# Rotary embedding on one core: the sine table is asked for ahead of the first two rows

## The chip, the core and the metric

The kernel runs on one core of a Trainium2 chip. Of the core's engines it uses VectorE (DVE in the profile) for the arithmetic, ScalarE (ACT) for a few conversions between float32 and float16, GpSimd (POOL) to issue most of the DMAs, and SyncE (SP) to issue the others. The core has 16 DMA engines, which all its DMAs share. TensorE (PE) has no work. The metric is the device time of one execution in microseconds (us); less is better.

## The reference

The input x has the shape (8, 2048, 16, 64) in float32: batch, position, head, and 64 numbers per head. The tables cos and sin have the shape (2048, 32). Each head's 64 numbers are two halves of 32, which are rotated against each other by the angle of the position:

```python
x1 = x[..., :head_dim // 2]
x2 = x[..., head_dim // 2:]
cos = cos[None, :, None, :]
sin = sin[None, :, None, :]
out1 = x1 * cos - x2 * sin
out2 = x1 * sin + x2 * cos
return np.concatenate([out1, out2], axis=-1)
```

x and the output have 67.1 MB each, a table 256 KB. Three operations per number of x stand against one read and one write of it.

## The kernel before, in words

**Tiles.** The 2048 positions of a batch are laid on 128 partitions, 16 consecutive positions ("rows", j) on each. A batch is one tile `xt` of 128 x 16 x 16 x 64 in float16 (4096 KB); five such buffers exist (`NBUF = 5`), so that batch b and batch b + 5 share one. The load (line 52) converts float32 to float16 on its way, and the stores (lines 60, 100, 130, 132) convert back.

**Arithmetic.** `rotate` makes three VectorE instructions per batch: line 73 multiplies the swapped halves with the sine table, whose first half has its sign turned (`v`), line 79 multiplies the tile in place with the cosine table, and line 81 adds `v`. The tables that VectorE reads, `sin_h` and `cos_h`, are float16. ScalarE makes them from the float32 tables: `sin_h` in two instructions (lines 88 and 89), `cos_h` in one (line 90).

**The head.** The first two rows of batch 0 (`JA = 2`, 1024 KB of float32) come by a way of their own. SyncE loads them in float32 into the tile `head` (line 36), and ScalarE converts them into the buffer of batch 0 (line 84). POOL's load of batch 0 brings only rows 2 to 15. `rotate` is called for rows 0 and 1 first, and then for rows 2 to 15. At the end of the kernel the tile `head` is used once more: ScalarE converts the last two rows of batch 7 into it (line 140), and SyncE stores them (line 141) behind the part of batch 7 that line 130 stores.

**Queues.** SyncE issues four DMAs, in the order head, sine table, cosine table, and the last rows at the end. The profile calls their queue q1 (hardware_dynamic). POOL issues everything else, and that queue is q0 (software_dynamic). POOL's order is: the loads of batches 0 to 3; the store of row 0 of batch 0 (line 100); the load of batch 4; the stores of batch 0 from row 1 on and of batch 1; the loads of batches 5 and 6; the stores of batches 2 and 3; the load of batch 7; the stores of batches 4 to 6; and batch 7 in two parts, rows 0 to 8 (line 130) and rows 9 to 13 (line 132). A load into a buffer that is used again waits until the store out of it has landed. A store waits for the last addition (line 81) of its rows.

Within q1 each DMA is cut into pieces of one row of memory per partition: 8192 bytes for the head, 2048 bytes for a table, eight pieces on each of the 16 DMA engines. In q0 a load's piece is counted at the float16 it writes (28672 bytes for batch 0, 32768 for the others).

Of the kernel before, what the change touches and what calls it, by code (L numbers as in the profile page):

```python
# [1 line left out]

# [4 lines left out]


@with_exitstack  # L10
def kernel(
    ctx: ExitStack,
    tc: tile.TileContext,
    x: bass.AP,
    cos: bass.AP,
    sin: bass.AP,
    out: bass.AP,
):
    nc = tc.nc
    f16 = mybir.dt.float16  # L20
    f32 = mybir.dt.float32

    B, S, H, D = x.shape
    Dh = D // 2
    P = nc.NUM_PARTITIONS
    J = S // P
    NBUF = 5

    const_pool = ctx.enter_context(tc.tile_pool(name="rope_const", bufs=1))
    io_pool = ctx.enter_context(tc.tile_pool(name="rope_io", bufs=NBUF))  # L30
    tmp_pool = ctx.enter_context(tc.tile_pool(name="rope_tmp", bufs=1))

    JA = 2
    head = const_pool.tile([P, JA, H, D], f32)
    x0 = x[0].rearrange("(p j) h d -> p j (h d)", j=J)
    nc.sync.dma_start(  # L36
        out=head.rearrange("p j h d -> p (j h d)"),
        in_=x0[:, 0:JA, :].rearrange("p j f -> p (j f)"),
    )
    sin_f = const_pool.tile([P, J, Dh], f32)  # L40
    cos_f = const_pool.tile([P, J, Dh], f32)
    cos_h = const_pool.tile([P, J, Dh], f16)
    sin_h = const_pool.tile([P, J, D], f16)
    nc.sync.dma_start(out=sin_f, in_=sin.rearrange("(p j) d -> p j d", j=J))  # L44
    nc.sync.dma_start(out=cos_f, in_=cos.rearrange("(p j) d -> p j d", j=J))

    loads = []

    def load(b):
        xt = io_pool.tile([P, J, H, D], f16)  # L50
        j0 = JA if b == 0 else 0
        dma = nc.gpsimd.dma_start(  # L52
            out=xt[:, j0:J, :, :].rearrange("p j h d -> p (j h d)"),
            in_=x[b].rearrange("(p j) h d -> p j (h d)", j=J)[:, j0:J, :].rearrange("p j f -> p (j f)"),
        )
        loads.append(dma)
        return xt

    def store(b, xt, j0=0):
        return nc.gpsimd.dma_start(  # L60
            out=out[b].rearrange("(p j) h d -> p j (h d)", j=J)[:, j0:J, :].rearrange("p j f -> p (j f)"),
            in_=xt[:, j0:J, :, :].rearrange("p j h d -> p (j h d)"),
        )

    def rotate(xt, j0, j1):
        v = tmp_pool.tile([P, J, H, D], f16)
        n = j1 - j0
        js = slice(j0, j1)
        shape = [P, n, H, 2, Dh]
        sin_b = sin_h[:, js, :].rearrange("p j (e d) -> p j e d", e=2).unsqueeze(2).to_broadcast(shape)  # L70
        cos_b = cos_h[:, js, :].unsqueeze(2).to_broadcast([P, n, 2 * H, Dh])
        xe = xt[:, js, :, :].rearrange("p j h (e d) -> p j h e d", e=2)
        nc.vector.tensor_mul(  # L73
            out=v[:, js, :, :].rearrange("p j h (e d) -> p j h e d", e=2),
            in0=xe[:, :, :, ::-1, :],
            in1=sin_b,
        )
        xw = xt[:, js, :, :].rearrange("p j h (e d) -> p j (h e) d", d=Dh)
        nc.vector.tensor_mul(out=xw, in0=xw, in1=cos_b)  # L79
        xa = xt[:, js, :, :].rearrange("p j h d -> p (j h d)")  # L80
        nc.vector.tensor_add(out=xa, in0=xa, in1=v[:, js, :, :].rearrange("p j h d -> p (j h d)"))  # L81

    tiles = [load(b) for b in range(NBUF - 1)]
    nc.scalar.copy(  # L84
        out=tiles[0][:, 0:JA, :, :].rearrange("p j h d -> p (j h d)"),
        in_=head.rearrange("p j h d -> p (j h d)"),
    )
    nc.scalar.copy(out=sin_h[:, :, Dh:D], in_=sin_f)  # L88
    nc.scalar.mul(out=sin_h[:, :, 0:Dh], in_=sin_f, mul=-1.0)  # L89
    nc.scalar.copy(out=cos_h, in_=cos_f)  # L90
    rotate(tiles[0], 0, JA)
    def part(b, j0, j1):
        return (
            out[b].rearrange("(p j) h d -> p j (h d)", j=J)[:, j0:j1, :].rearrange("p j f -> p (j f)"),
            tiles[b][:, j0:j1, :, :].rearrange("p j h d -> p (j h d)"),
        )

    def store_rows(b, j0, j1):
        dst, src = part(b, j0, j1)
        return nc.gpsimd.dma_start(out=dst, in_=src)  # L100

    first = store_rows(0, 0, 1)
    tc.add_manual_dep(
        first.ins,
        loads[NBUF - 2].ins.name,
        mybir.DependencyInfo(mybir.DependencyClass.NoSync, mybir.DependencyReason.DATA),
        reason="order of the ring",
    )
    tiles.append(load(NBUF - 1))
    tc.add_manual_dep(  # L110
        loads[NBUF - 1].ins,
        first.ins.name,
        mybir.DependencyInfo(mybir.DependencyClass.NoSync, mybir.DependencyReason.DATA),
        reason="order of the ring",
    )
    for b in range(B):
        rotate(tiles[b], JA if b == 0 else 0, J)
        if b < B - 1:
            st = store(b, tiles[b], 1 if b == 0 else 0)
            if b == 0:  # L120
                tc.add_manual_dep(
                    st.ins,
                    first.ins.name,
                    mybir.DependencyInfo(mybir.DependencyClass.NoSync, mybir.DependencyReason.DATA),
                    reason="order of the ring",
                )
        if b + NBUF < B:
            tiles.append(load(b + NBUF))
    dst, src = part(B - 1, 0, 9)
    gate = nc.gpsimd.dma_start(out=dst, in_=src)  # L130
    dst, src = part(B - 1, 9, J - JA)
    rest = nc.gpsimd.dma_start(out=dst, in_=src)  # L132
    tc.add_manual_dep(
        rest.ins,
        gate.ins.name,
        mybir.DependencyInfo(mybir.DependencyClass.NoSync, mybir.DependencyReason.DATA),
        reason="order of the ring",
    )
    dst, src = part(B - 1, J - JA, J)
    nc.scalar.copy(out=head.rearrange("p j h d -> p (j h d)"), in_=src)  # L140
    end = nc.sync.dma_start(out=dst, in_=head.rearrange("p j h d -> p (j h d)"))
    tc.add_manual_dep(
        end.ins,
        gate.ins.name,
        mybir.DependencyInfo(mybir.DependencyClass.Sync, mybir.DependencyReason.DATA),
        reason="the last rows go out behind this part",
    )


# [1 line left out]
_INS = ['x', 'cos', 'sin']  # L151
_OUTS = [((8, 2048, 16, 64), 'float32')]


# [23 lines left out]
```

## Time and profile before

| | |
|---|---|
| time, median of 3 runs | 317.52 us (316.82 to 317.85) |
| profiled execution, first to last instruction (span) | 315.70 us |
| outside the span, median less span | 1.82 us |
| VectorE busy | 209.1 us in 27 instructions |
| ScalarE busy | 6.8 us |
| POOL busy | 9.9 us |
| moved by q0 (counted at the destination) | 99.09 MB |
| moved by q1 (counted at the destination) | 2.62 MB |
| read from HBM, written to HBM | 67.63 MB, 67.11 MB |
| issue to landing: head, sine table, cosine table | 4.8, 13.5 and 32.0 us |

The profiled execution has no time of its own beside its span: what the device time has more, the start ahead of the first instruction and the end behind the last one, is taken as the difference to the median of the runs.

A page of the profile gives busy times, shares of the DMA engines in slices of the span, the chain of work that ended last, and groups of instructions with the idle time before them and what ended that. The DMA share of a stretch is the time of all DMA pieces that start in it, divided by 16 engines and by the length of the stretch. It can be a little over 1, because a piece is counted where it starts and neighbouring pieces of one engine overlap by some hundredths of a us. A share near 1 means that no DMA engine stood still. "Another core or an unknown queue" in the chain is time for which the profile found no releaser.

### The profile page before, as it was taken

To read this page: it belongs to the slowest core of one execution; us is meant where nothing else is said; L and a number is where in the kernel's file an instruction comes from. 1 tells how busy PE (TensorE), PEld (TensorE's weight loads), DVE (VectorE), ACT (ScalarE), POOL (GpSimd) and SP (SyncE) were. 2 spreads that over 40 slices of the span, in tenths; PEclk is the share of its full clock that TensorE was granted. 3 is DMA by queue.
4 is the path that set the end of the run, shared out by engine and by line. 5 is a ranking of instruction groups with operands and counts; after the bars stand their busy time and mean duration, and the time that the engine had idled before them with its cause. 6 is when DMAs were issued, how large, how long until landed. Compare 5 with 4: busy or idle time off the path is not lost.

```text
span 315.7 us, 122 instructions
## 1 busy us (share of the span) xinstructions
DVE 209.1 (66%) x27; ACT 6.8 (2%) x6; POOL 9.9 (3%) x22
## 2 busy tenths in 40 slices
DVE  0010699999999999999999999994009994000000
ACT  4100000000000000000000000000000002000000
POOL 3000100000000000001000000100000001000000
DMA  9899999999999989999999999999999999999998
GB/s 277 183 262 208 199 220 245 199 199 199 266 199 199 498 374 523 399 332 241 224 199 199 390 407 399 399 531 266 199 249 482 399 399 515 415 399 399 432 434 330
DMA packets 3168, 101.71 MB, mean 322 GB/s; under 512 B 352, under 2 KB 352, under 8 KB 736
## 3 DMA queue, kind: packets, MB, share of 16 engines
q0 software_dynamic: 2592, 99.09, 98.1%
q1 hardware_dynamic: 576, 2.62, 2.3%
HBM read 67.63 MB, written 67.11 MB: 427 GB/s over the span
## 4 chain that ended last, share of the span: by engine, by line
DVE 25%; DMA 22%; issue 18%; another core or an unknown queue 17%; POOL 1%; ACT 1%; SPq 0%; POOLq 0%; DVEq 0%; ACTq 0%
DMA xt<-in_x_dram 12%; DMA cos_f<-in_cos_dram 10%; DVE xt L79 8%; DVE xt L81 8%; DVE v L73 8%; ACT head L140 1%; POOL out_dram L60 1%; POOL xt L52 0%; ACT cos_h L90 0%; SPq L44 0%; SPq L36 0%; POOLq L52 0%; POOLq L60 0%; DVEq L73 0%
## 5 line engine op out<-in xcount | busy, mean ns | idle before, releaser
L73 DVE TENSOR_TENSOR v<-xt,sin_h 128x16384 f16<-128x16384 f16 (+2 forms) x9 | 69.7, 7744 | 36.8 <-DMA xt<-in_x_dram 20.7
L79 DVE TENSOR_TENSOR xt<-xt,cos_h 128x16384 f16<-128x16384 f16 (+2 forms) x9 | 69.7, 7744 | 17.5 <-ACT cos_h L90 17.2
L81 DVE TENSOR_TENSOR xt<-xt,v 128x16384 f16<-128x16384 f16 (+2 forms) x9 | 69.7, 7744 | 0.3
L52 POOL DMA_DIRECT2D xt<-in_x_dram x8 | 4.4, 557 | 111.1 <-DMA out_dram<-xt 110.3
L140 ACT CAST head<-xt 128x2048 f32<-128x2048 f16 x1 | 1.9, 1897 | 229.5 <-DVE xt L81 229.5
L60 POOL DMA_DIRECT2D out_dram<-xt x7 | 3.7, 535 | 63.9 <-DVE xt L81 63.9
L130 POOL DMA_DIRECT2D out_dram<-xt x1 | 0.5, 531 | 46.3 <-DVE xt L81 46.3
L84 ACT CAST xt<-head 128x2048 f16<-128x2048 f32 x1 | 1.9, 1897 | 3.6 <-DMA head<-in_x_dram 3.6
L100 POOL DMA_DIRECT2D out_dram<-xt x1 | 0.5, 541 | 33.5 <-DVE xt L81 33.5
L84 ACT ACT_TABLE_LOAD x1 | 1.3, 1283 | 0.7 <-PEq L162 0.7
L90 ACT CAST cos_h<-cos_f 128x512 f16<-128x512 f32 x1 | 0.6, 618 | 17.8 <-DMA cos_f<-in_cos_dram 17.8
L88 ACT CAST sin_h<-sin_f 128x512 f16<-128x512 f32 x1 | 0.6, 617 | 7.2 <-DMA sin_f<-in_sin_dram 7.2
L89 ACT ACTIVATE sin_h<-sin_f 128x512 f16<-128x512 f32 x1 | 0.6, 624 | 0.0
L132 POOL DMA_DIRECT2D out_dram<-xt x1 | 0.5, 531 | 0.0
L162 POOL MEMSET const-float32-0.0<- 128x1 f32 x1 | 0.1, 99 | 0.2 <-issue 0.2
L162 POOL MEMSET const-bfloat16-1.0<- 128x1 bf16 x1 | 0.1, 102 | 0.0
L162 POOL MEMSET const-float32-1.0<- 128x1 f32 x1 | 0.1, 99 | 0.0
L162 POOL MEMSET const-uint8-127<- 128x1 uint8 x1 | 0.1, 99 | 0.0
## 6 DMA issues: line engine op xcount, KB each, us to landing
xt<-in_x_dram POOLq DMA_DIRECT2D x7, 4096.0 KB, 41.3
out_dram<-xt POOLq DMA_DIRECT2D x1, 7680.0 KB, 61.6
out_dram<-xt POOLq DMA_DIRECT2D x1, 4608.0 KB, 42.4
xt<-in_x_dram POOLq DMA_DIRECT2D x1, 3584.0 KB, 22.3
out_dram<-xt POOLq DMA_DIRECT2D x1, 2560.0 KB, 47.9
head<-in_x_dram SPq DMA_DIRECT2D x1, 1024.0 KB, 4.8
out_dram<-head SPq DMA_DIRECT2D x1, 1024.0 KB, 8.4
out_dram<-xt POOLq DMA_DIRECT2D x1, 512.0 KB, 47.1
```

The source lines that it names most:

```text
L52: dma = nc.gpsimd.dma_start(out=xt[:, j0:J, :, :].rearrange("p j h d -> p (j h d)"), in_=x[b].rearrange("(p j) h d -> p j (h d)", j=J)[:, ...
L60: return nc.gpsimd.dma_start(out=out[b].rearrange("(p j) h d -> p j (h d)", j=J)[:, j0:J, :].rearrange("p j f -> p (j f)"), in_=xt[:, j0:J ...
L73: nc.vector.tensor_mul(out=v[:, js, :, :].rearrange("p j h (e d) -> p j h e d", e=2), in0=xe[:, :, :, ::-1, :], in1=sin_b,)
L79: nc.vector.tensor_mul(out=xw, in0=xw, in1=cos_b)
L81: nc.vector.tensor_add(out=xa, in0=xa, in1=v[:, js, :, :].rearrange("p j h d -> p (j h d)"))
L84: nc.scalar.copy(out=tiles[0][:, 0:JA, :, :].rearrange("p j h d -> p (j h d)"), in_=head.rearrange("p j h d -> p (j h d)"),)
L88: nc.scalar.copy(out=sin_h[:, :, Dh:D], in_=sin_f)
L89: nc.scalar.mul(out=sin_h[:, :, 0:Dh], in_=sin_f, mul=-1.0)
L90: nc.scalar.copy(out=cos_h, in_=cos_f)
L100: return nc.gpsimd.dma_start(out=dst, in_=src)
L130: gate = nc.gpsimd.dma_start(out=dst, in_=src)
L140: nc.scalar.copy(out=head.rearrange("p j h d -> p (j h d)"), in_=src)
```

## The change

SyncE's first two requests change places: the sine table is asked for first, then the head rows, then the cosine table. Nothing else is edited. The scheduler that sets each engine's order then also moves ScalarE's instructions: the two that make `sin_h` come first, then the conversion of the head rows, then `cos_h`. Before, the conversion of the head came first. The load of ScalarE's table, which stands ahead of its first instruction, stays first. The orders on VectorE and POOL are the same as before.

```diff
     JA = 2
     head = const_pool.tile([P, JA, H, D], f32)
     x0 = x[0].rearrange("(p j) h d -> p j (h d)", j=J)
-    nc.sync.dma_start(
-        out=head.rearrange("p j h d -> p (j h d)"),
-        in_=x0[:, 0:JA, :].rearrange("p j f -> p (j f)"),
-    )
     sin_f = const_pool.tile([P, J, Dh], f32)
     cos_f = const_pool.tile([P, J, Dh], f32)
     cos_h = const_pool.tile([P, J, Dh], f16)
     sin_h = const_pool.tile([P, J, D], f16)
     nc.sync.dma_start(out=sin_f, in_=sin.rearrange("(p j) d -> p j d", j=J))
+    nc.sync.dma_start(
+        out=head.rearrange("p j h d -> p (j h d)"),
+        in_=x0[:, 0:JA, :].rearrange("p j f -> p (j f)"),
+    )
     nc.sync.dma_start(out=cos_f, in_=cos.rearrange("(p j) d -> p j d", j=J))
```

## The prediction

> **What bounds the kernel now.** I read the slices and the DMA queues first, then the chain, then the windows, then the order in time of the first 36 us. Slices and queues of the page:
>
> ```profile
> DVE  0010699999999999999999999994009994000000
> DMA  9899999999999989999999999999999999999998
> q0 software_dynamic: 2592, 99.09, 98.1%
> q1 hardware_dynamic: 576, 2.62, 2.3%
> ```
>
> VectorE idles in the first tenth, in a stretch before the last batch, and at the end; the DMA engines never do, and the two queues together take 100.4% of 16 engines' span. The chain of waits ends like this, in its summary:
>
> ```profile
> DVE 25%; DMA 22%; issue 18%; another core or an unknown queue 17%; POOL 1%; ACT 1%; SPq 0%; POOLq 0%; DVEq 0%; ACTq 0%
> ```
>
> It names VectorE and a 10% share for the cosine table's DMA, but a chain follows releases: it cannot see that a request was released while its queue still had work. That has to be taken from the windows (length, busy times, granted clock, DMA share, GB/s):
>
> ```profile
> 0.00:1.70 1.70, 0.00 (x0) 0.96 (x1) 0.65 (x5) 1.00 0.00 0
> 1.70:2.60 0.90, 0.00 (x0) 0.32 (x1) 0.90 (x3) 1.00 1.03 164
> 2.60:4.80 2.20, 0.00 (x0) 0.00 (x0) 0.91 (x2) 1.00 0.96 398
> 4.80:5.30 0.50, 0.00 (x0) 0.00 (x0) 0.00 (x0) 1.00 1.15 389
> 5.30:14.00 8.70, 0.00 (x0) 1.90 (x1) 0.00 (x0) 1.00 1.01 223
> ...
> 33.00:82.00 49.00, 47.48 (x8) 0.62 (x1) 1.61 (x3) 1.00 0.98 207
> ...
> 264.00:314.50 50.50, 0.00 (x0) 1.67 (x1) 1.02 (x2) 1.00 0.98 415
> 314.50:315.70 1.20, 0.00 (x0) 0.00 (x0) 0.00 (x0) 1.00 0.00 0
> ```
>
> From 1.7 to 314.5 us the share is about 1: the time is 1.7 us of start, 312.8 us of DMA pieces, 1.2 us of end. What the change can move is therefore the idle time of DMA engines and the speed of pieces, not the chain. The start, in order of time:
>
> ```profile
> 0.74 0.37 SPq L36 DMA_DIRECT2D head<-in_x_dram  x1
> 1.16 0.42 SPq L44 DMA_DIRECT2D sin_f<-in_sin_dram  x1
> 1.25 2.26 POOL L52 DMA_DIRECT2D xt<-in_x_dram  x4 [0.81 <-PEq L173]
> 1.63 0.42 SPq L45 DMA_DIRECT2D cos_f<-in_cos_dram  x1
> 5.58 1.90 ACT L84 CAST xt<-head 128x2048 f16<-128x2048 f32 x1 [3.56 <-DMA head<-in_x_dram]
> 14.68 0.62 ACT L88 CAST sin_h<-sin_f 128x512 f16<-128x512 f32 x1 [7.20 <-DMA sin_f<-in_sin_dram]
> 15.86 1.22 DVE L73 TENSOR_TENSOR v<-xt,sin_h 128x2048 f16<-128x2048 f16 x1 [15.86 <-ACT sin_h L89]
> 33.63 0.62 ACT L90 CAST cos_h<-cos_f 128x512 f16<-128x512 f32 x1 [17.81 <-DMA cos_f<-in_cos_dram]
> 34.28 1.22 DVE L79 TENSOR_TENSOR xt<-xt,cos_h 128x2048 f16<-128x2048 f16 x1 [17.20 <-ACT cos_h L90]
> ```
>
> The trace's records of single DMA pieces fill this in. q1's first piece starts at 1.73 us, 0.99 after its issue. q0's first pieces start between 5.28 and 5.68, and by then q1 has moved 76.7 KB of the 98.3 KB per engine that head and tables have. From then on each engine takes one piece of q0 (2.13 us for batch 0, 2.43 later) and one of q1 (0.08 to 0.10 for 2 KB) in turn. About 12.2 pieces per engine were left of q1, its four-byte completion writes among them, and 8 rounds of 2.2 us and 4 of 2.53 bring the cosine table to 5.3 + 17.6 + 10.1 = 33 us; it landed at 33.6.
>
> **The change part by part.**
>
> *SyncE's order.* The sine request starts at 0.74 (before 1.16) and the head's at about 1.16 (before 0.74). 0.37 + 0.42 us of issue are the same in either order, so the cosine request stays at 1.63, and the store at the end (306.43) is untouched. Cost 0: no request of this queue is late for anything but its own data.
>
> *The first pieces.* An engine's first 8 KB piece took on average 0.89 us (0.63 to 1.27 for the first fifteen records), the steady one 0.31: 0.58 us per engine is start-up that carries no bytes. After the change a 2 KB piece bears it: 0.58 + 8 x 0.084 puts the end of the sine pieces at 1.73 + 1.25 = 2.98. The head's pieces can start at 1.16 + 0.99 = 2.15, so they should be in line already. Bounds: the start-up could shrink away (-0.58), or be paid a second time by the head (+0.58). I take 0, because the nearest row is the table behind the head in the window 4.80:5.30, where 2 KB pieces follow 8 KB pieces with no gap (share 1.15).
>
> *Work ahead of q0.* Until 5.28 the engines have only q1, which holds 98.3 KB per engine, 8 x 0.31 + 16 x 0.084 + 0.58 = 4.4 us of work from 1.73 on, to 6.1. It cannot run dry before q0 comes, in either order. So the bytes moved before q0 starts are the same, and what is left over is the same work in other pieces. Cost 0. If that cover went, each us of idle engines before 5.28 would be a us of the result.
>
> *Leftover pieces.* By 5.28 to 5.68 the sine table and 60 KB of an engine's 64 KB of head should be done: about 0.6 of a head piece, one completion and 9 cosine pieces are left, 10.6 instead of 12.2. The last head piece waits one or two turns of 2.13: the head lands at 7.5 to 10 (before 5.5), the cosine table at 5.3 + 17.6 + 2.6 x 2.53 = 29.5, about 4 us sooner. A turn costs what its bytes cost: pieces of q0 that start 2.20 apart with a 2 KB piece between, and 2.13 long, leave 0.07 for it. An 8 KB piece at 0.31 has the same rate, so no cost.
>
> [...]
>
> *ScalarE and VectorE.* The sine table lands near 3.3 (2.98 and the 0.35 from last head piece to landing), its two conversions of 0.62 end near 4.6; the head's 1.90 end at 9.4 to 12, and line 73 starts then rather than at 15.86. Line 79 still waits for the cosine table, near 30.2 instead of 34.28. All of rotate, back to back until 217 us, moves about 4 us forward. What hides this is the queue: the store of row 0 is issued at 37.06 but its pieces start at 82.05, the store of batch 0 60.04 against 102.6, that of batch 1 86.2 against 120.7, the loads of batches 5, 6 and 7 follow landings with about 18 us of pieces still queued, batch 7's multiplication waits for its load (237.53), and batch 7's store is issued at 263.97 against 294.6. VectorE may be some 18 us earlier or later without the DMA engines noticing. Worth 0.
>
> *Slow pieces.* Most 32768-byte pieces took 2.43 us, but between 42 and 82 us whole rounds took up to 3.05; over the loads of batches 2 and 3 the excess is 0.22 + 0.71 us, elsewhere 0.1. The page does not say why. Earlier VectorE work overlaps other pieces, so this may change: bounds -1.0 (all gone) to +1.0 (as much again), taken 0, as most loads show none.
>
> Sum: 0 on 315.70 of span; the 1.82 us between that and the median, start and end outside the span, are carried over (the runs themselves differ by 1.03). Predicted: 317.5.
>
> **The rivals.** Two results within 0.3% (0.95 us) can hardly be told from no change by a measurement of this kernel.
>
> *Front counts.* If the wait of VectorE for the cosine table (17.20 us in the last line above) bounded the end, 4 us sooner would give 313.5. For it: the chain passes there. Against: DMA share 1 throughout and 45 us between the first store's issue and its pieces.
>
> *An empty gap behind the sine table (slower).* If the head's pieces started only after the sine table had landed, engines would idle from 2.98 to 3.3 + 0.99 = 4.3: 1.3 us, 318.8. It is slower by more than 0.3% from 0.95 us of idle engines ahead of 5.3. For it: 256 KB cover little latency. Against: the 4.80:5.30 row.
>
> *Slow rounds go or grow.* 316.5 if all of the excess goes, 318.5 with as much again; with the first pieces' 0.58 in the same direction 315.9 and 319.1. For it: the spread of the three runs is as large. Against: nothing in the edit touches these loads.
>
> **How the numbers follow.** No difference 0.62. Front counts 0.05, and slow rounds and start-up together beyond the bound downward 0.13: faster 0.18. The gap 0.12, slow rounds upward 0.08: slower 0.20. The range leaves out Front counts and the far ends of the others: 316.4 (1.1 below) to 318.9 (the gap).
>
> **What would show it.** Right: windows with a DMA share near 1 from 1.7 to the end; the sine table landing by 4 us, the head at 6 to 10, the cosine table at 28 to 31; VectorE's idle time behind its first multiplication about as long as now; the store of row 0 issued near 33 and landing near 84 as before. Wrong: a DMA share well under 1 between 1.7 and 5.3; q0's first piece much off 5.3; the load of batch 3 ending more than 1 us off 82.6; or any stretch later with idle DMA engines, which would mean that POOL's issues, not the bytes, set its end.

## The result, and the profile after

The changed kernel took 316.63 us (median of 6 runs, 316.44 to 317.13), against 317.67 us (6 runs, 316.82 to 318.02) for the kernel before on the same chip. The ratio is 0.9972, with a 95% interval of 0.9961 to 0.9983. That is within the 0.3% that the prediction called no difference, but the whole interval lies below 1. Two later measurements of the same kernel gave 0.9984 (0.9974 to 0.9994) and 0.9989 (0.9980 to 0.9998). So there is a gain, of 0.3 to 0.9 us by these ratios. The 316.63 us lie near the lower end of the forecast range, 316.4 to 318.9.

The page of the changed kernel, slices and DMA queues:

```profile
DVE  0105999999999999999979999980009993000000
DMA  9899999999999899999999999999999999999998
q0 software_dynamic: 2592, 99.09, 98.2%
q1 hardware_dynamic: 576, 2.62, 2.1%
```

In slices, the row of the DMA engines is as full as before. VectorE's work starts earlier and its idle stretch ahead of the last batch is longer. The windows (length, busy times, clock, DMA share, GB/s):

```profile
1.70:2.60 0.90, 0.00 (x0) 0.32 (x1) 0.90 (x3) 1.00 0.77 223
2.60:4.80 2.20, 0.00 (x0) 1.15 (x2) 0.91 (x2) 1.00 1.06 438
...
33.00:82.00 49.00, 48.79 (x7) 0.00 (x0) 1.08 (x2) 1.00 0.97 211
...
264.00:314.50 50.50, 0.00 (x0) 0.65 (x1) 0.00 (x1) 1.00 0.98 415
```

In the first stretch 223 GB/s moved in place of 164, in the second 438 in place of 398, and from 33 to 82 us 211 in place of 207. The last stretch is the same. The share of 0.77 in the first stretch says that the engines were not full there. Before, the start-up stood in long opening pieces (share 1.03); now a part of it stands as idle time between short ones. The chain of waits, in its summary, has hardly changed (DMA 22% and an unknown queue 17% before):

```profile
DVE 25%; DMA 20%; another core or an unknown queue 19%; issue 18%; POOL 1%; ACT 1%; SPq 0%; POOLq 0%; DVEq 0%; ACTq 0%
```

The start, in order of time:

```profile
0.74 0.38 SPq L40 DMA_DIRECT2D sin_f<-in_sin_dram  x1
1.17 0.43 SPq L41 DMA_DIRECT2D head<-in_x_dram  x1
1.64 0.42 SPq L45 DMA_DIRECT2D cos_f<-in_cos_dram  x1
3.46 0.62 ACT L88 CAST sin_h<-sin_f 128x512 f16<-128x512 f32 x1 [1.44 <-DMA sin_f<-in_sin_dram]
7.99 1.90 ACT L84 CAST xt<-head 128x2048 f16<-128x2048 f32 x1 [3.38 <-DMA head<-in_x_dram]
9.92 1.23 DVE L73 TENSOR_TENSOR v<-xt,sin_h 128x2048 f16<-128x2048 f16 x1 [9.92 <-ACT xt L84]
26.14 0.62 ACT L90 CAST cos_h<-cos_f 128x512 f16<-128x512 f32 x1 [16.25 <-DMA cos_f<-in_cos_dram]
26.79 1.23 DVE L79 TENSOR_TENSOR xt<-xt,cos_h 128x2048 f16<-128x2048 f16 x1 [15.64 <-ACT cos_h L90]
29.57 0.54 POOL L100 DMA_DIRECT2D out_dram<-xt  x1 [26.06 <-DVE xt L81]
```

VectorE's line 79 starts 7.5 us sooner (34.28 before), and 1 us of that, at most, reaches the end. Where it does, two marks show: POOL's load of batch 5 waits for the landing of batch 0's store, and SyncE's last store waits for that of line 130. Before:

```profile
122.19 0.53 POOL L52 DMA_DIRECT2D xt<-in_x_dram  x1 [35.44 <-DMA out_dram<-xt]
...
306.43 0.35 SPq L141 DMA_DIRECT2D out_dram<-head  x1
```

After:

```profile
121.16 0.53 POOL L52 DMA_DIRECT2D xt<-in_x_dram  x1 [41.89 <-DMA out_dram<-xt]
...
305.39 0.35 SPq L141 DMA_DIRECT2D out_dram<-head  x1
```

The first mark is 1.03 us sooner, the second 1.04. From 122 us on the two executions are the same; between the marks lie 184.24 and 184.23 us. In the nine other profiles of the table below the distance is 184.2 to 184.3 as well. So what differs in time between these profiles happens ahead of the landing of batch 0's store.

To see what, I took three terms from the records of single DMA pieces: when the last pieces of batch 1's load end (mean of 16 engines; by then SyncE's three requests are done), how much longer than 2.432 us the pieces of batches 2 and 3 took (sum per engine), and how far the slowest engine ends behind the mean of all in the store of batch 6.

| profile | batch 1 loaded, us | excess, us | lag, us | load of batch 5 issued, us | ratio of its measurement |
|---|---|---|---|---|---|
| before | 42.64 | 0.96 | 0.30 | 122.19 | |
| before, again | 42.62 | 0.61 | 0.43 | 121.91 | 1.0001 |
| before, one row of VectorE | 42.57 | 0.39 | 0.39 | 121.62 | 1.0004 |
| after | 42.48 | 0.22 | 0.18 | 121.16 | 0.9972 |
| after, again | 42.44 | 1.07 | 0.29 | 122.10 | 0.9984 |
| after, third | 42.45 | 0.41 | 0.74 | 121.87 | 0.9989 |
| after, cosine late | 42.45 | 0.47 | 0.24 | 121.46 | 0.9972 |
| cosine, head, sine | 42.67 | 0.47 | 0.77 | 122.18 | 1.0003 |
| the same, again | 42.41 | 0.57 | 0.25 | 121.51 | 0.9987 |
| quarter of sine first | 42.85 | 0.73 | 0.39 | 122.34 | 0.9994 |
| sine, cosine, head | 42.94 | 0.19 | 1.33 | 122.74 | 1.0034 |

For the first pair the terms are -0.16, -0.74 and -0.12, together the 1.02 us. The table is complete in this sense: in all eleven profiles the load of batch 5 is issued 78.25 to 78.37 us after the sum of the three terms. Only the first term goes with the order, and not without exception: it is alike in the three profiles with the head first and in the four of the changed kernel's order, but cosine, head, sine gave 42.67 and 42.41.

### The profile page after: what moved, and what is told of

It reads as the page before. It is cut to its first block, busy times and chain, and to the rows that moved or that the text cites. A ratio compares the mean times of both kernels' runs of the same rounds, so it can differ in the third digit from the quotient of the medians.

```text
span 314.7 us, 122 instructions
## 1 busy us (share of the span) xinstructions
DVE 209.1 (66%) x27; ACT 6.8 (2%) x6; POOL 9.9 (3%) x22
## 4 chain that ended last, share of the span: by engine, by line
DVE 25%; DMA 20%; another core or an unknown queue 19%; issue 18%; POOL 1%; ACT 1%; SPq 0%; POOLq 0%; DVEq 0%; ACTq 0%
DMA xt<-in_x_dram 12%; DVE xt L81 8%; DVE xt L79 8%; DVE v L73 8%; DMA cos_f<-in_cos_dram 8%; ACT head L140 1%; POOL out_dram L60 1%; POOL xt L52 0%; ACT cos_h L90 0%; SPq L41 0%; SPq L40 0%; POOLq L52 0%; POOLq L60 0%; DVEq L73 0%
## 5 line engine op out<-in xcount | busy, mean ns | idle before, releaser
L100 POOL DMA_DIRECT2D out_dram<-xt x1 | 0.5, 541 | 26.1 <-DVE xt L81 26.1
```

## The experiments

Each measurement has 11 or 12 runs of the edited kernel (7 of the one with the cosine table late) beside 15 to 33 of the kernel before on the same chip. The comparisons were made at four times, and the kernel before took 317.32, 316.88, 317.36 and 317.36 us in them, so only ratios of one comparison are set side by side. A diff shows the lines edited in the changed kernel, shortened by "...", unless it says otherwise.

**The changed kernel again (no edit).**

> The changed kernel once more, for a second profile. Theory A (start-up: the first piece on each DMA engine now has 2 KB, and less start-up is lost ahead of the first piece of POOL's queue; the rest of the gain is the chance with which slow rounds of pieces fall): about 0.9 us faster than before, 316.4 to 317.2; the load of batch 1 ends about 0.2 us sooner than in the profile of before, while the excess of slow pieces in the loads of batches 2 and 3 may be anything from 0 to 1 us. Theory B (VectorE's work, 7.5 us sooner, falls on other pieces and slows fewer): the same time, and the slow rounds at the same places as in the first profile after (one round near 78.5 us, 0.2 us of excess). Theory C (no difference but chance): within 0.3 us of before.

Measured: 316.91 us, 0.9984 (0.9974 to 0.9994). Its profiled execution is the slowest of its 11 runs, 317.39:

```profile
122.10 0.53 POOL L52 DMA_DIRECT2D xt<-in_x_dram  x1 [42.85 <-DMA out_dram<-xt]
...
306.37 0.35 SPq L141 DMA_DIRECT2D out_dram<-head  x1
```

The start is 0.20 us sooner than in the first profile of before, but the slow rounds are back, at the places that they had before (52 to 62, 72 to 82 us), although VectorE stands 7.5 us sooner. Time and start are those of Theory A. The slow rounds speak against Theory B, and the 0.74 us that the first pair differed by in them is not a property of the change.

**A quarter of the sine table ahead of the head.** The diff is against the kernel before.

```diff
+    nc.sync.dma_start(out=sin_f[:, 0:4, :], in_=...[:, 0:4, :])
     nc.sync.dma_start(out=head..., in_=x0[:, 0:JA, :]...)
-    nc.sync.dma_start(out=sin_f, in_=...)
+    nc.sync.dma_start(out=sin_f[:, 4:J, :], in_=...[:, 4:J, :])
     nc.sync.dma_start(out=cos_f, in_=...)
```

> The order of before (head, sine, cosine), but the first quarter of the sine table (512-byte pieces) is asked for ahead of the head, the other three quarters behind it. The cosine table lands at 33 to 35 us as before, so VectorE's work stands where it stood. Theory A: the first pieces take about 0.2 us rather than 0.89, 0.3 to 0.5 us gained, 317.1 to 317.3. Theory B: no gain from the start beyond 0.2 us and the slow rounds as before, 317.5. Theory C: 317.6.

Measured: 317.28 us, 0.9994 (0.9985 to 1.0002). The time lies within Theory A's range, but the kernel before took 317.32 in this comparison, so that no gain of 0.3 to 0.5 us is there, and the load of batch 1 ends later than before (42.85), not sooner. The first pieces are short (27 ns), but then the head's first pieces are slow again: its 8 KB pieces took 0.358 us on the mean of 128, where those behind a whole table took 0.317 in the first profile of the changed kernel and those that open the queue 0.387 in that of before. The eight pieces of 512 bytes start between 1.75 and 2.23 us, the head's first ones from 2.23 on. I read it so: not the size of the first piece counts, but how much work there is to cover the wait of the next request. This kernel also has one request more, with 1.5 KB pieces; what that adds to the 42.85 was not tested apart, so the reading is not shown by this run alone.

**The cosine table late.**

```diff
+    for _ in range(6):
+        nc.scalar.copy(out=sin_f, in_=cos_f)
+        nc.scalar.copy(out=cos_f, in_=sin_f)
     nc.scalar.copy(out=cos_h, in_=cos_f)
```

> The changed kernel with 12 more copies on ScalarE (of the cosine table to and fro) between the landing of the cosine table and its conversion, so that VectorE's line 79 starts near 34 us as before and not at 26.8. The requests are those of the changed kernel. Theory A: as the changed kernel, 316.4 to 317.2. Theory B: the slow rounds return, 0.6 to 0.7 us slower than the changed kernel, 317.2 to 317.5. Theory C: within 0.3 us of before.

Measured: 316.73 us, 0.9972 (0.9962 to 0.9982), beside 316.91 for the changed kernel in the same comparison. VectorE's line 79 stood even later than in the kernel before:

```profile
36.98 1.23 DVE L79 TENSOR_TENSOR xt<-xt,cos_h 128x2048 f16<-128x2048 f16 x1 [23.56 <-ACT cos_h L93]
...
39.75 0.54 POOL L103 DMA_DIRECT2D out_dram<-xt  x1 [36.24 <-DVE xt L81]
```

The gain stays with VectorE 10 us behind the changed kernel. Neither the chain from the table to VectorE nor VectorE's place beside the loads makes it.

**Sine, cosine, head.**

```diff
     nc.sync.dma_start(out=sin_f, in_=...)
+    nc.sync.dma_start(out=cos_f, in_=...)
     nc.sync.dma_start(out=head..., in_=x0[:, 0:JA, :]...)
-    nc.sync.dma_start(out=cos_f, in_=...)
```

> SyncE asks for sine, cosine, head. 2 KB pieces open the queue as in the changed kernel; both tables land by about 4 us and the head near 10, so VectorE runs from about 10 us, 17 us sooner than in the changed kernel. Theory A: as the changed kernel, 316.4 to 317.2. Theory B: VectorE's place moves again, so the slow rounds move, and the time goes off that of the changed kernel by 0.3 us or more in either direction. Theory C: within 0.3 us of before.

Measured: 318.86 us (316.85 to 319.63), 1.0034 (1.0017 to 1.0051). A miss for Theories A and C. Theory B's time came true, but not its reason: the slow rounds cost less than in any other profile of the table (0.19). The head landed at 26 us and not near 10, so VectorE began at 28 and not at 10:

```profile
1.64 0.42 SPq L42 DMA_DIRECT2D head<-in_x_dram  x1
...
26.45 1.90 ACT L84 CAST xt<-head 128x2048 f16<-128x2048 f32 x1 [21.40 <-DMA head<-in_x_dram]
28.38 1.23 DVE L73 TENSOR_TENSOR v<-xt,sin_h 128x2048 f16<-128x2048 f16 x1 [28.38 <-ACT xt L84]
```

The DMA queues from 0 to 4.3 us (pieces, MB, share) point at why:

```profile
q0 software_dynamic: 16, 0.46, 57.9%
q1 hardware_dynamic: 288, 0.52, 36.5%
```

and the same stretch of the changed kernel, with no line for POOL's queue:

```profile
q1 hardware_dynamic: 231, 0.97, 59.6%
```

POOL's pieces start at 3.38 us here, directly behind SyncE's first two requests (two tables, 17.7 pieces on the mean of the engines, with the 4-byte piece that each request ends with on each engine), while in the changed kernel they start at 5.15, again behind the pieces of the first two (table and head, 17.1). So POOL's queue was ready by 3.4 us here, and since its request starts at the same time in both (1.24 and 1.25 us), it was probably SyncE's run of pieces that held it off there. Two requests are not the rule: in the kernel before, POOL's pieces came after the head and 5 of the 8 sine pieces, 14.2 in all. From then on each of the head's eight pieces stands behind one of POOL's, and the head lands 24.8 us after its request (6.8 in the changed kernel). The mean of the engines ends as early as in other kernels (294.31 in the store of batch 6, before 294.80). But POOL's first pieces took anything from 2.13 to 3.31 us, and one engine stays 1.33 us behind the mean to the end. SyncE's last store goes out 0.45 us after the last piece of line 130's store on the slowest engine in the kernel before (305.98 and 306.43) and 0.44 us after it in the changed one (304.95 and 305.39); here it goes out at 306.99, 0.56 us later than before, where the earlier mean and the larger lag come to 0.54. That the lag makes the slower time is read from the profile; it was not varied by itself. The profiled execution, at 318.03 us, was one of the faster ones of its 12.

**The kernel before against itself (no edit).**

> The kernel before against itself, for a second profile. Theory A' (cover: the opening request pays a start-up of about half a us on each DMA engine, and a whole table ahead of the head, 0.67 us of pieces, hides the start-up of the head's own pieces; three profiles of kernels with the sine table first end the load of batch 1 0.16 to 0.20 us sooner on the mean of the engines than the one profile of before, 42.64): the load of batch 1 ends at 42.6 to 42.7 again. If it ends at 42.45, the gain at the start was chance. The slow rounds of the loads of batches 2 and 3 may cost anything from 0.2 to 1.0 us. Ratio within 0.1% of 1.

Measured: 316.90 us, 1.0001 (0.9992 to 1.0010), in the comparison in which the kernel before takes 316.88. The load of batch 1 ends at 42.62, as expected: a second profile of before has the start of the first. The slow rounds from 50 to 78 us are all but absent.

**Cosine, head, sine, twice.** The diff is against the changed kernel.

```diff
-    nc.sync.dma_start(out=sin_f, in_=...)
+    nc.sync.dma_start(out=cos_f, in_=...)
     nc.sync.dma_start(out=head..., in_=x0[:, 0:JA, :]...)
-    nc.sync.dma_start(out=cos_f, in_=...)
+    nc.sync.dma_start(out=sin_f, in_=...)
```

> The changed kernel with the two tables in each other's place: cosine, head, sine. VectorE's first line 73 now waits for the late table, and its rotation of rows 0 and 1 starts near 26.8 us as a whole. Theory A': which table opens is all the same, 316.5 to 316.9, the load of batch 1 ends at 42.4 to 42.5. If it matters what VectorE does between 10 and 27 us, the time leaves that of the changed kernel by 0.3 us or more.

> Cosine, head, sine once more, on the same chip as the changed kernel. Theory A': the same as the changed kernel within 0.1%, and the profile shows the start of the changed kernel (the load of batch 1 ending at 42.4 to 42.5) unless one engine lags, as in the first profile of this kernel. If it is again as slow as before while the changed kernel is faster, then which table opens does matter.

Measured: first 316.96 us, 1.0003 (0.9994 to 1.0012), with the profile of its slowest run (317.46): start 42.67 and a lag of 0.77. Then 316.96 us, 0.9987 (0.9979 to 0.9996), with a start of 42.41 and a lag of 0.25, beside 0.9989 for the changed kernel. The first was a miss, and the second in line with Theory A': within one comparison the two kernels with a table first cannot be told apart. One kernel on one chip thus gave 1.0003 and 0.9987: from one comparison to another a ratio moves by more than the half width of its interval, 0.0009.

**VectorE cut to one row.** The diff is against the kernel before.

```diff
     def rotate(xt, j0, j1):
         v = tmp_pool.tile([P, J, H, D], f16)
+        j1 = j0 + 1
         n = j1 - j0
```

> The kernel before with VectorE's work cut to one row of each rotation (the other rows are left as loaded, so the output lacks the rotation there); the DMAs and POOL's order are those of before. Theory V (the slow rounds come from VectorE's traffic in SBUF beside the loads): they go, 316.6 to 316.8, with little spread. Theory A' (they come from elsewhere, by chance): 317.2 to 317.5 with the spread of before, and slow rounds in the profile between 42 and 82 us.

Measured: 316.94 us, 1.0004 (0.9996 to 1.0013). VectorE's busy time fell from 209.1 us to 18.7:

```profile
DVE 18.7 (6%) x27; ACT 6.8 (2%) x6; POOL 9.9 (3%) x22
```

Yet neither the time changes nor the slow round at 79 us goes (2.82 us a piece; the view is explained at the next run):

```profile
q0 software_dynamic: 16, 0.52, 235.2%
```

VectorE does not bound the kernel, and Theory V falls for that round. Both ranges were missed, since the kernel before itself took 316.88 here. (The other slow rounds were absent in the kernel before too in this comparison, so this run says nothing of them.)

**Without the store of row 0.** The diff is against the changed kernel; the dependencies that ordered that store go with it.

```diff
-    first = store_rows(0, 0, 1)
     tiles.append(load(NBUF - 1))
...
-            st = store(b, tiles[b], 1 if b == 0 else 0)
+            st = store(b, tiles[b])
```

> The changed kernel without the separate store of row 0: batch 0 is stored as a whole behind the load of batch 4, which is therefore issued with the first four loads. In all six profiles so far the last round of batch 3's load, which the store of row 0 follows, was slow (2.5 to 3.1 us a piece instead of 2.43). Theory R (the store of row 0 behind it slows that round): the round at 79 us is as fast as the others and 0.2 to 0.5 us is gained, 316.1 to 316.6, unless a slow round then comes at the end of batch 4's load. If the round stays slow, its place in time or in the ring of requests is the cause, and the time is that of the changed kernel, 316.5 to 316.9.

Measured: 317.37 us, 1.0015 (1.0006 to 1.0023). Queue lines of a stretch in which just the 16 pieces of one round start give the mean of a piece: share times length. From 78.4 to 79.6 us, the last round of batch 3's load, in the kernel before (2.476 x 1.2 = 2.97 us):

```profile
q0 software_dynamic: 16, 0.52, 247.6%
```

and in the changed kernel (2.65 us):

```profile
q0 software_dynamic: 16, 0.52, 221.0%
```

Without the row 0 store, first the same stretch (2.44 us, the common time) and then 97.5 to 99.1 us, the last round of batch 4's load (3.20 us):

```profile
q0 software_dynamic: 16, 0.52, 203.1%
...
q0 software_dynamic: 16, 0.52, 199.7%
```

The slow round has moved with the store, to just ahead of POOL's first store, and costs 0.76 us there in place of 0.2 to 0.6. Theory R holds for the place, and its caveat came true: the time is worse. The round is not all of it: the last store goes out 184.53 us after the load of batch 5 here, 0.3 us more than in the profiles of the table.

**The changed kernel a third time (no edit).**

> The changed kernel a third time, since the two measurements so far were 0.9972 and 0.9984 of before, and the one of the cosine table first was 1.0003 on another chip. Theory A' (cover at the start): the load of batch 1 ends at 42.4 to 42.5 on the mean of the engines, and the ratio is about 0.999, the 0.2 us at the start out of 317; the rest of what was measured before came from slow rounds and the balance of the engines, which differ by chip and run. If the ratio is 0.998 or less again, more than the start belongs to the change.

Measured: 317.13 us, 0.9989 (0.9980 to 0.9998), with the expected 42.45.

**Row 0 stored by SyncE.** The diff is against the kernel without the row 0 store.

```diff
+    dst, src = part(0, 0, 1)
+    nc.scalar.copy(out=head[:, 0, :, :]..., in_=src)
+    nc.sync.dma_start(out=dst, in_=head[:, 0, :, :]...)
...
-            st = store(b, tiles[b])
+            st = store(b, tiles[b], 1 if b == 0 else 0)
```

> The changed kernel, with row 0 of batch 0 converted to float32 by ScalarE into the free head tile and stored by SyncE near 30 us, while POOL's queue is still loading; POOL stores rows 1 to 15 behind batch 4. Until now the round of loads just ahead of POOL's first store was slow wherever that store stood (0.2 to 0.6 us ahead of the row 0 store, 0.75 ahead of the whole batch). If the first write to the output pays, whoever issues it, the slow pieces move to about 31 us and none are left at 79 or 98; the time is that of the changed kernel or up to 0.4 us better. If the first store of POOL's queue pays, the slow round is the last of batch 4's load, as without the row 0 store, 0.3 to 0.5 us slower than the changed kernel.

Measured: 317.36 us, 0.9997 (0.9989 to 1.0006). SyncE's store goes out at 30.40 us, and no round near 31 us is slow; the one ahead of POOL's first store, at 99.5, takes 2.98 to 3.34 us a piece. From 99.2 to 100.2 us (3.12 us on the mean):

```profile
q0 software_dynamic: 16, 0.52, 312.4%
```

That is the second case of the forecast, with 0.23 us over the changed kernel in the same comparison rather than 0.3 to 0.5. A first write to the output by another queue does not take the cost away.

**The first store cut to two heads.** The diff is against the changed kernel; `store_from(b, f0, f1)` stores the numbers f0 to f1 of each partition.

```diff
-    first = store_rows(0, 0, 1)
+    first = store_from(0, 0, 2 * D)
...
-            st = store(b, tiles[b], 1 if b == 0 else 0)
+            st = store_from(0, 2 * D) if b == 0 else store(b, tiles[b])
```

> The changed kernel, with POOL's first store cut from row 0 of batch 0 (4096-byte pieces) to its first two heads (512-byte pieces); the rest of batch 0 follows with the store behind batch 4's load. The slow round ahead of POOL's first store cost 0.22 to 0.6 us with the row 0 store and 0.75 us with the whole batch. If the size of that first store sets it, the round at 79 us is slowed by less than 0.2 us and the time is 0.2 to 0.4 us under the changed kernel, 316.5 to 316.8 (0.997 to 0.998 of before). If it goes with the first store whatever its size, the round at 79 us costs 0.2 to 0.6 us as before, and the time is that of the changed kernel, about 0.9985.

Measured: 317.24 us, 0.9992 (0.9983 to 1.0001). Stretches 78.4 to 79.6 and 97.5 to 99.1 us:

```profile
q0 software_dynamic: 16, 0.52, 202.8%
...
q0 software_dynamic: 16, 0.52, 206.3%
```

The round at 79 is now at its common 2.43 us, as the first theory had it, but the next, larger store pays: 3.30 us a piece at 98. The first theory missed the time; the second has it within the interval, but not the place of the slow round. So 512-byte pieces did not pay here, and did not spare the next store either; 4 KB pieces paid 0.2 to 0.6 us, and the last round of batch 4's load stayed at 2.43 us a piece behind them, before and after. None of the kernels tried is clearly faster than the changed one.

## Why the prediction was right, and where it was not

**No difference beyond 0.3%.** It held, for the reason that it gave: the DMA share is 0.96 or more in each of the ten stretches from 2.60 to 314.50 us, before and after, and the run with one row of VectorE's work (18.7 us busy in place of 209.1, ratio 1.0004) shows that VectorE does not bound the kernel. The rival "Front counts" is out: VectorE came 7.5 us sooner, and the kernel in which it came 10 us later again kept the gain.

**The first pieces, bounds -0.58 to +0.58, taken 0.** This is the term that was mis-sized. It measures about -0.14: the load of batch 1 ends at 42.57 to 42.64 in three profiles with the head first (mean 42.61) and at 42.44 to 42.52 in six that open with sine, head, cosine (mean 42.47; besides the four of the table, 42.51 without the store of row 0 and 42.52 with the store of two heads; where SyncE stores row 0, that store falls into the stretch, and 42.96 cannot be compared).

The row that I took it from, tables that follow the head with no gap, was the right one to deny the rival of an empty gap, but its share of 1.15 was misread: a POOL piece that starts at 5.28 counts in it with its whole 2.13 us, and up to 5.27 the share is 0.90. It is the records of single pieces that show no gap there. After the change, too, 8 KB pieces follow 2 KB pieces at once (share 1.06 from 2.6 to 4.8 us).

If the second request's start-up is hidden by the first one's pieces, then only the opening pieces pay. In the first pair of profiles the 16 opening pieces took 0.87 us in place of 0.31 before, and 0.22 in place of 0.08 after. Of these 0.42 us only 0.16 are left when batch 1 is loaded: the pieces of head and tables take 4.17 us per engine after and 4.56 before, but those of batch 0's load 17.19 after and 17.05 before, and the rest is gaps. That the order moves the start is shown; that cover is the reason is how I read it.

**"Until 5.28 the engines have only q1."** The conclusion, that SyncE's bytes cannot run dry first, held. The reason was probably wrong: in the run with the two tables first POOL's queue is ready by 3.4 us, so that in the others SyncE's run of pieces seems to hold it off. On the mean 14.2 of SyncE's pieces per engine go ahead in the kernel before, 17.1 in the changed kernel and 17.7 with the two tables first. Then the queues take turns, about one piece each: in the six rounds of POOL's pieces from 7.5 to 20.6 us SyncE's queue has 0.75 to 1.19 pieces per engine and round before (mean 1.00), and 0.88 to 1.13 after (from 7.3 us on, mean 1.02).

**Leftover pieces and landings.** The sine table at 3.4 us (forecast 3.3) and the head at 8.0 (7.5 to 10) came as worked out. The cosine table came at 26.1, not 29.5: the head was out on all engines when POOL's first pieces started, and 9.9 pieces per engine were left where the sum has 10.6, of which the last landed after some nine turns. It cost nothing, since VectorE has the cover that was listed.

**Slow pieces, -1.0 to +1.0, taken 0.** In the first pair of profiles they make -0.74 of the -1.03. Over three profiles of each order they measure 0.22, 1.07 and 0.41 after and 0.96, 0.61 and 0.39 before (one with VectorE's work cut). That is no difference that these profiles can show. So it was in large part the draw that the first pair of profiles differed by 1 us, and it was luck that the range held the measured time so far from its middle: the bounds of this term, not its mechanism, reach there. Against this stand the ratios of the times, worth 0.3 to 0.9 us. The start explains some 0.14 of that. The rest is either slow rounds and lag that come less often with a table first, or the draw of the runs; six profiles do not settle it, and I leave it open.

**The signs.** Two of the signs of being wrong showed, both weakly: the share of 0.77 from 1.70 to 2.60 us, and the load of batch 3, whose last piece ends at 81.53 us, 1.0 us sooner than before (82.55). The first is the start-up; the second is mostly the draw of the slow rounds, as it ends at 82.47 and 82.25 in the other two profiles of the changed kernel.

**The chances.** Most of the chance on no difference was fair. With the start-up at its measured -0.14 us the middle would have been about 317.4 rather than 317.5.

## What to carry to other kernels

Here, with a DMA share of 0.96 or more from 2.6 to 314.5 us before and after, the order of the first requests moved little but the start-up ahead of the first steady pieces (0.14 us) and, in the profiles, the balance between the engines (a lag of 0.18 to 1.33 us). Look at the DMA share by windows before following the chain of waits, and mind that a long piece counts whole in the window where it starts. Try opening with a request of small pieces and the large one directly behind it: here, with 0.67 us of small pieces per engine in front (8 of 0.084 us), the load of batch 1 ended about 0.14 us sooner, and with 0.2 us (and one request more) it did not (42.85). That the work in front covers the start-up of the large request is my reading. Putting all small requests first cost 0.3% here: the large one then shared its turns with the bulk queue and landed at 26 us in place of 8, and in the profile one engine that is 1.3 us behind sets the end.

## What was not expected of the hardware

The last round of loads ahead of POOL's first store of 4 KB pieces or more was slow on all 16 engines at once: 2.65 to 3.03 us a piece on the mean in place of 2.43 in six profiles with a row 0 store of 4 KB pieces, 3.12 to 3.30 us in the three where the first such store has 60 to 64 KB pieces. It moved with that store and came once: before and after, the last rounds of the loads of batches 4 to 7 took 2.43 us a piece. Cutting VectorE's work (2.82 us) and an earlier write to the output through SyncE's queue (3.12 us) did not take it away. What causes it was not found.

A lag that an engine got in the first microseconds stayed in the order sine, cosine, head: the slowest engine is 1.07 us behind the mean at 23 us and 1.33 at 295.
